# Shifting the up projections' split weights inside their buffers, by 16 bytes a tile in block 1 and 4 bytes a tile in block 2

## The chip, the cores and the metric

The kernel runs on one core of a Trainium2 chip. The metric is the device time of one execution in microseconds (us), the median of the timed runs. Engines are named as the profile names them: PE is TensorE (PEld its weight loads), DVE is VectorE, ACT is ScalarE, POOL is GpSimd, SP is SyncE, which here issues the weights' DMAs.

## What is computed

Two transformer blocks stand one behind the other, with 512 tokens, a width of 1024 and all data in float32. The first mixes forgetting attention with chunked gating, the second mixes latent attention with chunked attention under a modulated norm. Both end in the same kind of feed-forward part, and that is what the change touches:

```python
def conv_ffn(x, w_up, conv_w, conv_b, w_down):       # block 1; block 2 is alike
    h = x @ w_up                                     # 512 x 1024 @ 1024 x 5632
    h = lax.conv_general_dilated(h, ...) + conv_b    # causal, 3 taps, by channel
    a, g = jnp.split(h, 2, axis=-1)
    return (jax.nn.silu(g) * a) @ w_down             # 512 x 2816 @ 2816 x 1024
```

## The kernel before

Activations lie transposed, features on the 128 partitions and the 512 tokens along the free axis. Every large product is made of three matmuls in fp32r: an operand is split into a rounded part and a rest (`hi`, `lo`), and hi*hi, hi*lo and lo*hi are added up in one bank of PSUM.

**Weights.** `make_plan` writes down every piece of weights in the order of its use: what is loaded, whether POOL or DVE makes the rest, where the split goes, and a number called `skew`. `load_split` handles one piece: SP's DMA brings 128 x 1024 floats into `wraw`, ACT copies them into `whi` (line 345), DVE or POOL writes the rest into `wlo` (line 346). `whi` and `wlo` have four buffers each, 128 x 1088 floats, and the split starts `skew` floats into the buffer. A buffer is 4352 bytes long on each partition, 17 times 256, so the four buffers of each pool start at the same place modulo 256 bytes. The built program puts them and the activations `xnh`, `xnl` (tiles of 4096 bytes) at 128 modulo 256. `weights` takes pieces in the plan's order and keeps two more than the matmuls need loaded (`LOOK` = 2).

**Products by features** (`gemm_fm`: up, down, w_qk, w_lat). The weights are the stationary operand, 128 x 128 a matmul, and the activations the moving one, 512 columns wide. One output tile of the up projection is one piece of weights: 8 steps along k, 3 matmuls each. `ffn_up` goes over the tiles in pairs, j and j + 22. Its first two pairs are made in two halves of 256 columns, the other 40 tiles in full width. All of `gemm_fm`'s pieces have skew 0.

**Products by tokens** (`gemm_tm`). Here the activations are stationary and the weights move. Where a piece is under 384 columns wide, its skew is 48 floats, 192 bytes; otherwise it is 0.

PE's order is the order of the code; each matmul loads its own stationary operand, also where it is the same as the one before.

Of the kernel before, what the change touches and what calls it, by code (L numbers as in the profile page):

```python
# [231 lines left out]
class Kernel:  # L232
# [41 lines left out]
    def make_plan(self):  # L274
        i, plan = self.i, []

        def fm(name, tiles, kt0=0, nk=KT, pool=False, last=None):
            for n in tiles:
                for p in self.fm_pieces(i[name], n, kt0, nk):
                    plan.append((p, pool, None, 0))  # L280
            if last:
                plan[-1] = plan[-1][:2] + (last, 0)

        def tm(name, n, nk=KT, pool=True, last=None, per=None):
            skew = SKEW // 4 if n < 384 else 0
            for p in self.tm_pieces(i[name], n, nk, per):
                plan.append((p, pool, None, skew))
            if last:
                plan[-1] = plan[-1][:2] + (last, 0)

        def parts(name, dest):
            for p in range(4):
                for g in range(2):
                    plan.append((i[name][p, g], False, dest.get((p, g)), 0))

        def ffn(up, down, last=None):
            for j in range(NF):
                fm(up, [j, j + NF])
            fm(down, range(KT), 0, NF, last=last)

        tm("w_v", 512, pool=False, per=1)
        tm("w_g1", 264, pool=False)
        fm("w_qk", [0, 4])
        fm("w_qk", [1, 5])
        tm("w_g0", 256, pool=False)
        tm("w_u", 512)
        fm("w_qk", [2, 6], pool=True)
        fm("w_qk", [3, 7], pool=True)

        parts("w_out", {(3, 1): ("mx", "mix", "mix")})  # L310
        ffn("w_up", "w_down", ("cv", "cv", "cv"))
        fm("w_lat", range(3))
        tm("w_ck0", 256, pool=False, last=("one", "m0", "m1"))
        tm("w_cq0", 288)
        tm("w_cv0", 256)

        def mla(c):
            tm(f"w_q{c}", 384, 2, False)
            tm(f"w_kn{c}", 256, 1, False)
            tm(f"w_kv{c}", 256, 1, False)  # L320

        for j, w in enumerate(("w_cq1", "w_ck1", "w_cv1")):
            if j == 2:
                mla(0)
            tm(w, 256)
        mla(1)
        parts("w_out_2", {(3, 0): ("one", "m3", "m4"), (3, 1): ("one", "m0", "m1")})
        ffn("w_up_2", "w_down_2")
        self.plan, self.loaded, self.taken = plan, [], 0
        self.ada_left, self.pools, self.before = [], {}, []  # L330

# [1367 lines left out]
```

## Time and profile before

| what | value |
|---|---|
| timed runs | 1245.37, 1245.84, 1248.73 us; median 1245.84 |
| the profiled execution | 1248.05 us, of them 1245.1 us from the first to the last instruction |
| PE busy | 1206.6 us, 97% of the span, 6730 matmuls |
| DVE, ACT, POOL busy | 803.4, 536.7, 173.0 us |
| mean granted clock of PE | 0.989 |
| up projection in full width, block 1 and 2 | about 261 to 478 us and 903 to 1120 us |
| down projections in full width | about 478 to 583 us and 1120 to 1225 us |

A matmul's row in the timeline gives when it began and how long it took to the modelled end. Matmuls overlap, so the time that one costs is the distance between two starts, called the pitch below, and not the duration in the row. Over a stretch, the pitch is the length of the stretch by the count of matmuls in it.

### The profile page before, as it was taken

To read this page: it belongs to the slowest core of one execution; us is meant where nothing else is said; L and a number is where in the kernel's file an instruction comes from. 1 tells how busy PE (TensorE), PEld (TensorE's weight loads), DVE (VectorE), ACT (ScalarE), POOL (GpSimd) and SP (SyncE) were. 2 spreads that over 40 slices of the span, in tenths; PEclk is the share of its full clock that TensorE was granted. 3 is DMA by queue.
4 is the path that set the end of the run, shared out by engine and by line. 5 is a ranking of instruction groups with operands and counts; after the bars stand their busy time and mean duration, and the time that the engine had idled before them with its cause. 6 is when DMAs were issued, how large, how long until landed. Compare 5 with 4: busy or idle time off the path is not lost.

```text
span 1245.1 us, 17452 instructions
## 1 busy us (share of the span) xinstructions
PE 1206.6 (97%) x6730; PEld 1048.7 (84%) x6730; DVE 803.4 (65%) x1538; ACT 536.7 (43%) x963; POOL 173.0 (14%) x202
## 2 busy tenths in 40 slices
PE   9989999899999999999998998999999999999998
PEld 6878878888888888888998997889988888888887
DVE  6656887587877777533656889766676566563221
ACT  5534554354344343322534556564554444442110
POOL 1255401210000000000264332301200000000000
PEclk9989999999999999999998999999999999999999
DMA  7311222146555566533121222110132222233330
GB/s 239 105 65 52 85 68 68 52 144 206 179 184 189 196 199 191 181 93 114 56 94 42 73 83 76 35 35 18 59 119 93 102 102 86 101 93 102 118 110 17
DMA packets 40034, 131.58 MB, mean 106 GB/s; under 512 B 4608, under 2 KB 5504, under 8 KB 39952
## 3 DMA queue, kind: packets, MB, share of 16 engines
q1 hardware_dynamic: 31536, 102.64, 25.7%
q10 hardware_dynamic: 8208, 27.27, 6.7%
q8 instruction: 52, 0.85, 0.3%
q0 software_dynamic: 208, 0.57, 0.2%
q14 instruction: 30, 0.25, 0.1%
HBM read 128.37 MB, written 2.10 MB: 105 GB/s over the span
## 4 chain that ended last, share of the span: by engine, by line
PE 83%; DVE 8%; POOL 4%; ACT 3%; issue 2%; DMA 1%; SPq 0%; POOLq 0%; ACTq 0%; DVEq 0%
PE mm L367 73%; PE s L367 4%; PE o L367 3%; PE s L603 2%; POOL wlo L346 1%; DVE wlo L346 1%; DMA x<-in_xT_dram 1%; ACT p L594 1%; ACT whi L345 0%; PE s L694 0%; DVE s L590 0%; DVE kl L668 0%; DVE nw L522 0%; PE mm L1639 0%; POOL gelu L1081 0%
## 5 line engine op out<-in xcount | busy, mean ns | idle before, releaser
L367 PE MATMUL mm<-xnh,whi 128*128 128x512 f32 (+1 forms) x832 | 313.4, 377 | 3.2 <-DVE nt L550 3.2
L367 PE MATMUL mm<-xnl,whi 128*128 128x512 f32 (+1 forms) x832 | 312.5, 376 | 1.9 <-DVE xnl L562 1.3
L367 PE MATMUL mm<-xnh,wlo 128*128 128x512 f32 (+1 forms) x832 | 311.9, 375 | 0.0
L346 DVE TENSOR_TENSOR wlo<-wraw,whi 128x1024 fp32r<-128x1024 f32 (+4 forms) x175 | 200.6, 1155 | 167.1 <-ACT whi L345 166.2
L345 ACT CAST whi<-wraw 128x1024 fp32r<-128x1024 f32 (+4 forms) x194 | 191.5, 991 | 259.2 <-PE mm L367 214.3
L367 PEld LDWEIGHTS mm<-xnh,whi 128*128 128x128 f32 x832 | 157.9, 190 | 30.8 <-issue 3.8
L367 PEld LDWEIGHTS mm<-xnl,whi 128*128 128x128 f32 x832 | 158.0, 190 | 29.8 <-DVE xnl L562 1.5
L367 PEld LDWEIGHTS mm<-xnh,wlo 128*128 128x128 f32 x832 | 157.8, 190 | 27.6
L367 PE MATMUL mm<-gh,whi 128*128 128x512 f32 (+1 forms) x384 | 141.7, 369 | 1.1 <-DVE x L936 0.6
L367 PE MATMUL mm<-gh,wlo 128*128 128x512 f32 (+1 forms) x384 | 141.4, 368 | 0.0
L367 PE MATMUL mm<-gl,whi 128*128 128x512 f32 (+1 forms) x384 | 141.4, 368 | 0.0
L728 DVE SCALAR_TENSOR_TENSOR cv<-mm,cols,cv 128x510 f32<-128x510 f32 (+1 forms) x176 | 130.5, 746 | 2.9 <-ACT cv L726 1.4
L367 PE MATMUL mm<-whi,xnh 128*128 128x256 f32 (+3 forms) x304 | 97.1, 319 | 0.7 <-ACT vv L1045 0.6
L367 PE MATMUL mm<-wlo,xnh 128*128 128x256 f32 (+3 forms) x304 | 94.1, 310 | 0.3 <-DVE wlo L346 0.3
L367 PE MATMUL mm<-whi,xnl 128*128 128x256 f32 (+3 forms) x304 | 93.8, 309 | 0.1
L997 DVE CUSTOM_DVE_ANT_0 wada<-wada,cs,cols 128x1024 f32<-128x1024 f32 x48 | 61.5, 1281 | 38.8 <-DMA wada<-in_w_ada_dram 38.8
L367 PEld LDWEIGHTS mm<-gh,whi 128*128 128x128 f32 x384 | 72.4, 189 | 13.6 <-DVE x L936 0.8
L367 PEld LDWEIGHTS mm<-gl,whi 128*128 128x128 f32 x384 | 72.4, 189 | 12.0
L367 PEld LDWEIGHTS mm<-gh,wlo 128*128 128x128 f32 x384 | 72.4, 189 | 11.9
L594 ACT ACTIVATE p<-s,st 128x128 f32<-128x128 f32 (+1 forms) x96 | 50.6, 528 | 66.5 <-DVE st L590 50.8
L367 PE MATMUL mm<-mix,whi 128*128 128x256 f32 (+1 forms) x288 | 74.8, 348 | 3.8 <-ACT vm L1567 2.6
L743 ACT ACTIVATE cv<-cv 128x512 f32<-128x512 f32 x44 | 27.8, 632 | 114.8 <-DVE cv L728 114.8
(311 smaller groups left out, 1877.7 us busy)
## 6 DMA issues: line engine op xcount, KB each, us to landing
wraw<-in_w_up_dram SPq DMA_DIRECT2D x88, 512.0 KB, 3.4
wada<-in_w_ada_dram ACTq DMA_DIRECT2D x48, 512.0 KB, 3.6
wraw<-in_w_down_dram SPq DMA_DIRECT2D x32, 512.0 KB, 3.5
wraw<-in_w_out_dram SPq DMA_DIRECT2D x16, 512.0 KB, 3.4
wraw<-in_w_down_dram SPq DMA_DIRECT2D x16, 384.0 KB, 3.2
wraw<-in_w_qk_dram SPq DMA_DIRECT2D x8, 512.0 KB, 3.5
wraw<-in_w_v_dram SPq DMA_DIRECT2D x8, 256.0 KB, 4.8
x<-in_xT_dram SPq DMA_DIRECT2D x8, 256.0 KB, 6.0
```

The costliest lines, as they stand in the source:

```text
L345: nc.scalar.copy(hi[:, :n], raw[:, :n])
L346: (nc.gpsimd if pool else nc.vector).tensor_tensor(out=lo[:, :n], in0=raw[:, :n], in1=hi[:, :n].bitcast(F32), op=ALU.subtract)
L367: self.nc.tensor.matmul(out, lhsT, rhs, start=start, stop=stop, **kw)
L594: nc.scalar.activation(out=p[:, :nk], in_=s[:, :nk], func=AF.Exp, bias=st[:, len(parts) - 1:len(parts)], scale=-1.0, accum_out=hd["sums"](qi))
L603: self.nc.tensor.transpose(s[:, c], p[:, c], self.ident)
L728: nc.vector.scalar_tensor_tensor(out=t[:, d:], in0=ps[:, :512 - d], scalar=w[2 - d], in1=t[:, d:], op0=ALU.mult, op1=ALU.add)
L743: nc.scalar.activation(out=gate, in_=gate, func=AF.Silu)
L997: nc.vector.tensor_tensor_reduce(out=w, in0=w, in1=self.cs, scale=1.0, scalar=self.col("b_ada_2", n), op0=ALU.mult, op1=ALU.add, accum_out ...
```

## The change

`ffn` gets a `step`, and after the two pieces of a pair have been put into the plan it gives each a skew of its own. With t the tile's place in the order of use, 0 to 43, the skew is `step * t` modulo `16 * step` floats. Block 1 has step 4, so the split weights start at 0, 16, 32 ... 240 bytes and then at 0 again; block 2 has step 1, so they start at 0, 4, 8 ... 60 bytes. `whi` and `wlo` of a piece share the offset. Tiles 0, 16 and 32 keep offset 0. In the built program every engine has the same instructions in the same order with the same waits; only the addresses in `whi` and `wlo` differ. The raw weights, the activations, the down projections and every other product stay where they were.

```diff
-        def ffn(up, down, last=None):
+        def ffn(up, down, step, last=None):
+
             for j in range(NF):
                 fm(up, [j, j + NF])
+                for n in (-2, -1):
+                    plan[n] = plan[n][:3] + (step * (2 * j + 2 + n) % (16 * step),)
             fm(down, range(KT), 0, NF, last=last)
...
-        ffn("w_up", "w_down", ("cv", "cv", "cv"))
+        ffn("w_up", "w_down", 4, ("cv", "cv", "cv"))
...
-        ffn("w_up_2", "w_down_2")
+        ffn("w_up_2", "w_down_2", 1)
```

## Rows read from the trace of the kernel before

**Rows 1.** The page: span, busy time by engine, chain that ended last.

```profile
span 1245.1 us, 17452 instructions
...
PE 1206.6 (97%) x6730; PEld 1048.7 (84%) x6730; DVE 803.4 (65%) x1538; ACT 536.7 (43%) x963; POOL 173.0 (14%) x202
...
PE 83%; DVE 8%; POOL 4%; ACT 3%; issue 2%; DMA 1%; SPq 0%; POOLq 0%; ACTq 0%; DVEq 0%
```

**Rows 2.** Stretches: length, busy time (instructions) of PE, PEld, DVE, ACT, POOL, clock, DMA.

```profile
266.00:470.00 204.00, 204.00 (x902) 169.01 (x901) 164.18 (x227) 85.27 (x114) 0.00 (x0) 1.00 0.58 188
906.00:1110.00 204.00, 204.00 (x902) 169.01 (x901) 127.59 (x155) 90.49 (x116) 0.00 (x0) 1.00 0.29 100
482.00:580.00 98.00, 98.00 (x434) 81.21 (x433) 46.39 (x67) 30.29 (x47) 0.00 (x0) 1.00 0.49 148
```

**Rows 3.** Timeline of PE, up projection of block 1: start, duration (us), instruction.

```profile
300.17 0.39 PE L367 MATMUL mm<-xnh,whi 128*128 128x512 f32 x1
300.40 0.39 PE L367 MATMUL mm<-xnl,whi 128*128 128x512 f32 x1
...
302.21 0.39 PE L367 MATMUL mm<-xnh,whi 128*128 128x512 f32 x1
```

**Rows 4.** Timeline of PE, w_v, full width, just after a wait.

```profile
18.84 0.50 PE L367 MATMUL mm<-wlo,xnh 128*128 128x512 f32 x1 [0.26 <-DVE wlo L346]
19.18 0.39 PE L367 MATMUL mm<-whi,xnl 128*128 128x512 f32 x1
19.41 0.40 PE L367 MATMUL mm<-whi,xnh 128*128 128x512 f32 x1
19.64 0.40 PE L367 MATMUL mm<-wlo,xnh 128*128 128x512 f32 x1
...
21.26 0.39 PE L367 MATMUL mm<-whi,xnl 128*128 128x512 f32 x1
21.49 0.39 PE L367 MATMUL mm<-whi,xnh 128*128 128x512 f32 x1
21.71 0.39 PE L367 MATMUL mm<-wlo,xnh 128*128 128x512 f32 x1
```

**Rows 5.** Timeline of PE, down projection of block 1, halves of 256 columns, all offsets 0.

```profile
595.63 0.28 PE L367 MATMUL mm<-gl,whi 128*128 128x256 f32 x1
...
597.07 0.28 PE L367 MATMUL mm<-gl,whi 128*128 128x256 f32 x1
```

**Rows 6.** Timeline of PE, w_ck0, 256 columns, moving weights at 192 bytes.

```profile
628.54 0.28 PE L367 MATMUL mm<-whi,xnh 128*128 128x256 f32 x1
...
630.81 0.28 PE L367 MATMUL mm<-whi,xnl 128*128 128x256 f32 x1
```

**Rows 7.** Timeline of PE, w_cv0, 256 columns, moving weights at 192 bytes.

```profile
650.51 0.28 PE L367 MATMUL mm<-wlo,xnh 128*128 128x256 f32 x1
...
652.39 0.28 PE L367 MATMUL mm<-whi,xnl 128*128 128x256 f32 x1
```

**Rows 8.** Timeline of PE, w_out_2, 512 columns, moving operand 64 bytes off the weights.

```profile
761.06 0.63 PE L367 MATMUL mm<-mix,whi 128*128 128x512 f32 x2
761.53 0.39 PE L367 MATMUL mm<-mix,wlo 128*128 128x512 f32 x1
761.76 0.62 PE L367 MATMUL mm<-mix,whi 128*128 128x512 f32 x2
762.22 0.40 PE L367 MATMUL mm<-mix,wlo 128*128 128x512 f32 x1
```

**Rows 9.** Groups in 266:470: count, busy us, mean ns, idle before (us) and its releasers.

```profile
L367 PE MATMUL mm<-xnh,whi 128*128 128x512 f32 x300 | 116.8, 389 | 0.0
L367 PEld LDWEIGHTS mm<-xnh,whi 128*128 128x128 f32 x301 | 56.5, 188 | 11.6
L346 DVE TENSOR_TENSOR wlo<-wraw,whi 128x1024 fp32r<-128x1024 f32 x38 | 45.1, 1219 | 1.5 <-ACT whi L345 1.4
L345 ACT CAST whi<-wraw 128x1024 fp32r<-128x1024 f32 x38 | 39.8, 1046 | 50.5 <-PE mm L367 32.6 <-DVE mod L997 18.0
...
L728 DVE SCALAR_TENSOR_TENSOR cv<-mm,cols,cv 128x510 f32<-128x510 f32 x39 | 29.0, 745 | 0.0
L728 DVE SCALAR_TENSOR_TENSOR cv<-mm,cols,cv 128x511 f32<-128x511 f32 x37 | 27.7, 748 | 0.9 <-ACT cv L726 0.8
```

**Rows 10.** The same columns, ACT in 628:665, splits written at an offset of 192 bytes.

```profile
L345 ACT CAST whi<-wraw 128x1024 fp32r<-128x1024 f32 x6 | 6.2, 1047 | 8.4 <-DMA wraw<-in_w_cv_dram 4.6 <-PE mm L367 3.9
```

## The prediction

> **What bounds the kernel now.** I read the page first, then stretches, then single rows of PE. The page says that PE is busy for 97% of the span and holds 83% of the chain that ended last [rows 1]. The second question is whether the touched stages are limited by PE alone. In both up projections PE is busy for all of a 204 us stretch, at clock 1.00 throughout (2.4 GHz, the upper of its two levels), and its group by form has no idle time before it [rows 2, 9]. DVE works 164.2 of the 204 us in block 1 and 127.6 in block 2, ACT 85 and 90 [rows 2]. So nothing but the pitch of the matmuls sets the end here, and the change can act by the pitch alone, unless it makes another engine late.
>
> The third question is what a matmul costs. From 300.17 to 302.21 there are nine pitches: 2.04 / 9 = 0.2267 us [rows 3]. The stretch agrees: 902 matmuls touch 204 us, and since each row is 389 ns long about 1.7 of these began before it, so 204 / 900.3 = 226.6 ns, in both blocks and, by 98 us and 434, in the down projection [rows 2, 9]. At 2.4 GHz, 512 columns are 213.3 ns, so 13.3 ns more are paid a matmul.
>
> This pitch is a rhythm that PE falls into, not a fixed price. After a wait the starts in w_v go 19.18, 19.41, 19.64 ... 21.26: nine pitches of (21.26 - 19.18) / 9 = 231.1 ns; from 21.49 on the pitch is 0.22 to 0.23 us again and stays so [rows 4]. The bout costs 9 x (231.1 - 226.7) = 40 ns. Once found, the rhythm holds through both up projections, over all four weight buffers.
>
> And the rhythm depends on where the two operands lie. At 256 columns with all operands at the same place modulo 256 bytes, 12 pitches take 1.44 us, 120.0 ns [rows 5]. Where the weights are skewed by 192 bytes I find 20 pitches in 2.27 us, 113.5 ns, in one product [rows 6], and 16 in 1.88 us, 117.5 ns, in another with the same addresses modulo 256 [rows 7]. So an offset between the two reads can change a matmul by up to 6.5 ns, and the same offset can give two rhythms.
>
> **The change, part by part.** No instruction is added, removed or moved.
>
> The matmuls concerned: a block's up projection has 40 tiles in full width, 24 matmuls each, 960, and 4 tiles in halves, 4 x 24 x 2 = 192. Tiles 0, 16 and 32 keep offset 0, so 38 x 24 = 912 and 3 x 48 = 144 a block are shifted, 1824 and 288 in all. One ns of pitch on the full ones is 1.8 us of time, 0.15%.
>
> *Full width, in rhythm.* The moving operand, and with it its place in memory, is what it was; the stationary one is read within the 226.7 ns beside it, 188 ns a load, with idle time before it [rows 9]. At 512 columns I have no row with an offset and a long run. The nearest with equal operands is 226.7 [rows 3]. The only rows with an offset are in block 2's output projection, where the moving operand lies 64 bytes off the weights: 1.16 us from 761.06 to 762.22 for five pitches, 232 ns, but in a run broken by attention, in which equal operands show 231 too [rows 4, 8]. The floor is read from the slope: from 113.5 to 226.7 ns, 256 columns more cost 113.2 ns, so the best rhythm at 256 costs 0.443 ns a column and so does the one that the up projection has now. I read this as a price of streaming the moving operand with nothing on top; the 120.0 at 256 has 6.5 ns on top, the 231 to 232 some 4.4. An offset can take away only what is on top, and here there is nothing left. So the bounds are 0 and +4.4 ns a matmul, 0 to +8.0 us (1824 x 4.4), with a gain below 0 left to a rival. I take 0: the row with the same moving operand, the same width and an unbroken run is the 226.7 one.
>
> *Full width, at a change of tile.* Offsets differ between neighbouring tiles, so PE may have to find its rhythm anew 88 times. Bounds: nothing, as at every change of buffer now, or a bout of 40 ns each, 88 x 0.040 = 3.5 us [rows 4]. I take 1 us, nearer to nothing, since each step is 4 or 16 bytes, against the wait of [rows 4] that starts a bout.
>
> *Halves.* 288 matmuls at 120.0 ns may become 117.5 or 113.5, -0.7 or -1.9 us [rows 5 to 7]; or stay. I take -0.7.
>
> *ACT and DVE.* They write the splits at offsets that are no longer multiples of 64 bytes. ACT's copy takes 1047 ns at an offset of 192 bytes and 1046 at 0 [rows 9, 10]. DVE already writes at 4 and at 8 bytes past a tile's start in the convolution, 511 and 510 columns, in 748 and 745 ns [rows 9]. So 0. Cover, if that fails: DVE has 204 - 164.2 = 39.8 us idle in block 1's stretch, 1.05 us for each of its 38 splits of 1219 ns; they would have to become almost twice as long before PE waits [rows 2, 9].
>
> The sum: 0 + 1.0 - 0.7 + 0 = +0.3 us. The profiled execution took 1248.05 us, span 1245.1, and would take 1248.3; it stands 2.2 us above the median of the runs, 1245.84. Against that median I predict 1246.1 us.
>
> The skill has a rule on this. Under "Who interferes with whom", the Trainium skill's page "SBUF — State Buffer" gives TensorE two independent read ports, one for the moving operand and one for weight loads, and says that PE waits on nobody; by it an offset does nothing anywhere, and the sum would be 0. The trace does not bear out its general form, since 120.0 and 113.5 ns stand side by side for the same work at different offsets [rows 5, 6], but those are matmuls with hardly any time beside the load.
>
> **Rivals.**
>
> *The rhythm breaks (slower).* The 226.7 may need both operands at the same place modulo 256 bytes. At other offsets PE would stay in what [rows 4] show only in passing, 231.1 ns. For: the same offset of 192 bytes has two rhythms at 256 columns, the slower one 4 ns above the other over a run of 16 pitches [rows 6, 7]; the rows with an offset at 512 columns show 232 [rows 8]. Against: those come after interruptions, and at 512 columns the load has slack. Price 4.4 x 1824 = +8.0 us, less 0.7: 1253.1 us. It decides from the point at which more than half the offsets lose the rhythm: +4 us, 1249.8.
>
> *The offset takes something off (faster).* What helped the 256-column products by 2.5 to 6.5 ns [rows 5 to 7] may be an event a matmul, whatever its width. The pitch would fall to 224.2 or 220.2: 1824 x 2.5 = 4.6 us or 1824 x 6.5 = 11.9 us, and 0.7 to 1.9 in the halves; 1240.6 or 1232.1 us. Against it stands the slope above. For it: full columns at 2.4 GHz are 213.3 ns, so 13.3 remain to be explained, and I only inferred that they belong to the stream. It may hold for some offsets and not for others. The Trainium skill's page "TensorE: Matmul & The Clock Gate", under "Back-to-back issue gap", gives N / 2.4 + 2.5 ns, 215.8 at 512 columns; by it, as an estimate, 10.9 ns a matmul are there to be had, 19.9 us. No run of fp32r here comes near it.
>
> *The change is inert.* Hi and lo share their offset and the moving operand is fixed, so if only the moving stream sets the pitch nothing changes, in the halves either: 1245.8. This is in the forecast's band.
>
> **How the numbers follow.** The forecast with the inert case gets 0.50, the broken rhythm 0.32, the gain 0.18. The forecast's own band is 1245.8 - 1.9 = 1243.9 up to 1245.8 + 3.5 = 1249.3. About 0.3%, 3.7 us, is what a measurement of this kernel can tell from no change: below 1242.1 is faster, above 1249.5 slower. So same 0.50, slower 0.32, faster 0.18. The range for 8 in 10 is 1241 to 1254: it takes in the forecast, the whole price of the broken rhythm with room for the spread of runs, and of the gain only its weak edge; some 0.15 is left out below and 0.03 above.
>
> **What would show it.** Right: in both up projections some 902 matmuls touch a stretch of 204 us, and starts are 226 or 227 ns apart at every offset, with at most a few longer ones at a tile's start. Broken rhythm: about 885 in the stretch (204 / 231.1 + 1.7), and pitches between 224 and 236 within a tile, perhaps only at some offsets; block 1 and block 2 need not agree. A gain: 912 to 928 matmuls. ACT's row at 1046 ns and DVE's at 1219 would show the writes untouched. The forecast is wrong if PE shows idle time before whi or wlo, or if tiles with one offset have a pitch of their own.

## The result and the profile after

The changed kernel takes 1261.22 us (median of 1256.49, 1261.08, 1261.37 and 1261.82), the kernel before in the same comparison 1246.72: a ratio of 1.0099, 95% interval 1.0085 to 1.0113, or 12.3 us (10.6 to 14.1). It is slower by 1%, outside the range that I gave. The profiled execution took 1261.82 us, its span is 1260.1 us; 1245.1 before [rows 1].

The page of the changed kernel: span, busy time, and the chain that ended last.

```profile
span 1260.1 us, 17452 instructions
...
PE 1219.2 (97%) x6730; PEld 1051.4 (83%) x6730; DVE 804.8 (64%) x1538; ACT 538.3 (43%) x963; POOL 173.1 (14%) x202
...
PE 82%; DVE 8%; POOL 4%; ACT 3%; issue 2%; DMA 1%; SPq 0%; POOLq 0%; ACTq 0%; DVEq 0%
```

The same instructions, the same bound; PE is busy for 12.6 us longer. The stretches of [rows 2], the second one moved to where block 2's up projection now runs:

```profile
266.00:470.00 204.00, 204.00 (x882) 165.37 (x882) 163.10 (x223) 85.21 (x112) 0.00 (x0) 1.00 0.57 189
920.00:1124.00 204.00, 204.00 (x880) 164.92 (x879) 123.31 (x149) 85.69 (x111) 0.00 (x0) 1.00 0.29 100
482.00:580.00 98.00, 98.00 (x434) 81.14 (x433) 49.17 (x72) 30.45 (x48) 0.00 (x0) 1.00 0.46 142
```

Where 902 matmuls touched 204 us, 882 and 880 do, at the same granted clock of 1.00 and with no gap in PE's work. The down projection, whose weights did not move, keeps its 434 in 98 us. So the pitch has grown in the two up projections and nowhere else.

How much that costs in all is read from the chain that ended last. Its two longest pieces are unbroken work of PE: from block 1's up projection through the down projection, and the same in block 2. Columns: start (us), length (us), what, count. The third row shown is the piece just ahead of block 2's, 39 matmuls in halves. Before:

```profile
247.42 343.72 PE mm L367 x1599
...
883.35 4.78 PE mm L367 x39
...
891.78 341.21 PE mm L367 x1577
```

and after:

```profile
248.67 348.52 PE mm L370 x1599
...
891.63 6.23 PE mm L370 x39
...
901.51 346.42 PE mm L370 x1577
```

The same 1599 matmuls take 4.80 us more, the same 1577 take 5.21 us more: 10.0 us of the span's 15.0. The other 5.0 us lie outside these pieces, and 1.45 of them are in sight: the 39 matmuls in halves take 6.23 us instead of 4.78. The experiments come back to that.

The groups of 266 to 470 us, as [rows 9]:

```profile
L370 PE MATMUL mm<-xnh,whi 128*128 128x512 f32 x294 | 115.9, 394 | 0.0
L370 PEld LDWEIGHTS mm<-xnh,whi 128*128 128x128 f32 x294 | 55.2, 188 | 12.8
...
L349 DVE TENSOR_TENSOR wlo<-wraw,whi 128x1024 fp32r<-128x1024 f32 x37 | 44.2, 1218 | 2.8 <-ACT whi L348 2.6
L348 ACT CAST whi<-wraw 128x1024 fp32r<-128x1024 f32 x37 | 38.6, 1044 | 53.2 <-PE mm L370 53.2
```

A matmul's row is 394 ns long instead of 389, but a weight load is still 188 ns, and the splits are written in 1218 and 1044 ns (1219 and 1046 before). Writing at these offsets costs DVE and ACT nothing, and PE still has no idle time.

Last, the starts of neighbouring tiles in block 1, the first matmul of each. A tile is 24 matmuls, so the distance between two rows by 24 is the tile's mean pitch:

```profile
284.25 0.40 PE L370 MATMUL mm<-xnh,whi 128*128 128x512 f32 x1
...
289.85 0.39 PE L370 MATMUL mm<-xnh,whi 128*128 128x512 f32 x1
...
323.25 0.40 PE L370 MATMUL mm<-xnh,whi 128*128 128x512 f32 x1
...
328.71 0.39 PE L370 MATMUL mm<-xnh,whi 128*128 128x512 f32 x1
...
334.15 0.39 PE L370 MATMUL mm<-xnh,whi 128*128 128x512 f32 x1
...
339.60 0.39 PE L370 MATMUL mm<-xnh,whi 128*128 128x512 f32 x1
...
345.19 0.40 PE L370 MATMUL mm<-xnh,whi 128*128 128x512 f32 x1
```

The tile at 128 bytes: 289.85 - 284.25 = 5.60 us, 233.3 ns a matmul. The one at 240 bytes: 5.46, 227.5. At 0: 5.44, 226.7. At 16: 5.45, 227.1. At 32: 5.59, 232.9. Read in this way, every offset has a pitch that comes back each time it is used (mean ns in full width; the sequence of single pitches inside a tile repeats too):

| block 1, bytes | 16 | 32 | 48 | 64 | 80 | 96 | 112 | 128 | 144 | 160 | 176 | 192 | 208 | 224 | 240 | 0 |
|---|---|---|---|---|---|---|---|---|---|---|---|---|---|---|---|---|
| pitch | 227.0 | 233.0 | 233.2 | 233.1 | 231.8 | 233.9 | 233.1 | 233.4 | 233.4 | 233.0 | 229.8 | 229.1 | 233.1 | 233.3 | 227.5 | 226.7 |

| block 2, bytes | 4 | 8 | 12 | 16 | 20 | 24 | 28 | 32 | 36 | 40 | 44 | 48 | 52 | 56 | 60 | 0 |
|---|---|---|---|---|---|---|---|---|---|---|---|---|---|---|---|---|
| pitch | 232.3 | 230.9 | 229.7 | 233.4 | 232.7 | 231.1 | 234.8 | 233.3 | 234.3 | 233.4 | 230.4 | 233.3 | 233.0 | 233.1 | 230.4 | 228.1 |

More than half stand near 233.3, which is 6.7 ns above 226.7. At 0 and 240 the first few pitches are long (238, 232, 230 at 240 bytes; 230, 236, 229, 232, 231 at 0 in block 2) and then the rhythm of 226.7 is found again.

One thing stands out: 16 bytes costs nothing in block 1, where the tile ahead is at 0, and 6.7 ns a matmul in block 2, where the tile ahead is at 12.

### The profile page after: what moved, and what is told of

Its sections match the earlier page's. It is cut to its first block, busy times and chain, and to the rows that moved or that the text cites. A ratio compares the mean times of both kernels' runs of the same rounds, so it can differ in the third digit from the quotient of the medians.

```text
span 1260.1 us, 17452 instructions
## 1 busy us (share of the span) xinstructions
PE 1219.2 (97%) x6730; PEld 1051.4 (83%) x6730; DVE 804.8 (64%) x1538; ACT 538.3 (43%) x963; POOL 173.1 (14%) x202
## 4 chain that ended last, share of the span: by engine, by line
PE 82%; DVE 8%; POOL 4%; ACT 3%; issue 2%; DMA 1%; SPq 0%; POOLq 0%; ACTq 0%; DVEq 0%
PE mm L370 72%; PE s L370 4%; PE o L370 3%; PE s L606 2%; DVE wlo L349 1%; POOL wlo L349 1%; ACT whi L348 1%; ACT p L597 1%; DMA x<-in_xT_dram 0%; DVE nw L523 0%; DVE s L593 0%; DMA wraw<-in_w_g_dram 0%; DVE kl L671 0%; PE s L697 0%; PE mm L1642 0%
## 5 line engine op out<-in xcount | busy, mean ns | idle before, releaser
L370 PE MATMUL mm<-xnh,whi 128*128 128x512 f32 (+1 forms) x832 | 316.7, 381 | 3.2 <-DVE nt L553 3.2
L370 PE MATMUL mm<-xnl,whi 128*128 128x512 f32 (+1 forms) x832 | 316.0, 380 | 1.9 <-DVE xnl L565 1.3
L370 PE MATMUL mm<-xnh,wlo 128*128 128x512 f32 (+1 forms) x832 | 315.3, 379 | 0.0
```

What stands on the lines that cost most here:

```text
L370: self.nc.tensor.matmul(out, lhsT, rhs, start=start, stop=stop, **kw)
```

## The experiments

Three theories were set against each other. **A**: the pitch depends on the distance between the moving and the stationary operand, modulo 256 bytes, and on nothing else of the address. **B**: the change disturbs the clock, and that is part of the loss. **C**: it is the change of offset from tile to tile that costs, each tile having to find its rhythm anew. Spans are compared with the 1245.1 us of before; the pieces of the chain with 343.72 (1599 matmuls) and 341.21 (1577). In the first two kernels below, the block that is left alone has its piece back to 0.01 us; so one execution is enough to read a piece from, though not to compare totals.

### One block at a time

In one kernel only block 1's tiles keep their steps of 16 bytes, in the other only block 2's their steps of 4.

```diff
-                    plan[n] = plan[n][:3] + (step * (2 * j + 2 + n) % (16 * step),)
+                    plan[n] = plan[n][:3] + (skew(2 * j + 2 + n),)
```

with, for block 1 and for block 2 alone (in floats, by the tile's place t; the kernels below differ in this line),

```diff
+            skew = {"w_up": lambda t: 4 * (t % 16), "w_up_2": lambda t: 0}[up]
...
+            skew = {"w_up": lambda t: 0, "w_up_2": lambda t: t % 16}[up]
```

> The stagger of 16 bytes in block 1 alone. The changed kernel's span was 15.0 us longer: 4.8 us of it in block 1's up projection, 5.4 in block 2's, 4.8 elsewhere (1.3 at the start, the rest where the granted clock fell to half at other places). Theory A, the pitch: only block 1's up projection is slower, by 4.8 us, so about 1251.5 us against 1246.7. Theory B, the rest belongs to the change too (a later block 2 meets the clock's falls in another way): 1251.5 plus up to 4.8, about 1254 to 1256.

> The stagger of 4 bytes in block 2 alone. Theory A, the pitch: slower by 5.4 us, about 1252.1 us, with block 1's up projection back at 226.7 ns a matmul. Theory B, as in the run of block 1 alone: nothing ahead of block 2 is changed, so the clock's falls ahead of it stand where they stood and the time is 1252 as well; the two theories differ by the other run.

Block 1 alone: 1255.14 us, ratio 1.0068 (1.0045 to 1.0092). Block 2 alone: 1254.7 us, ratio 1.006 (1.0036 to 1.0084). The two long pieces of the chain, block 1 alone:

```profile
251.10 348.52 PE mm L370 x1599
...
899.31 341.21 PE mm L370 x1577
```

and block 2 alone:

```profile
249.34 343.71 PE mm L370 x1599
...
892.29 346.43 PE mm L370 x1577
```

Each block loses its own 4.80 or 5.22 us and the other block nothing. The two effects are independent and add up, to within 0.02 us of what the whole change costs in these pieces. A and C both want that. The timed differences, 8.5 and 7.5 us, lie above 4.8 and 5.2, though only block 1's interval (5.6 to 11.5 us) leaves its own piece out. Block 1's 1255.14 us falls where B had put it; block 2's 1254.7 is above the 1252 that both theories gave.

### Offsets that differ by 256 bytes

Every second tile of block 1 stands at 256 bytes, every second one of block 2 at 128.

```diff
+            skew = {"w_up": lambda t: 64 * (t % 2), "w_up_2": lambda t: 32 * (t % 2)}[up]
```

> Odd tiles of the up projections lie 256 bytes further in block 1, 128 bytes further in block 2. Theory A, the distance between the operands modulo 256 bytes sets the pitch: block 1 stays at 226.7 ns in every tile (902 matmuls in a stretch of 204 us) although each tile has another offset than the one before; block 2 has 233.4 ns in its odd tiles and, after some matmuls of 224 to 236, 226.7 in its even ones, together some 230.5. Theory C, it is the change of offset from tile to tile that costs: both blocks lose some 5 us alike.

```profile
249.13 343.72 PE mm L370 x1599
...
892.03 344.43 PE mm L370 x1577
```

One execution: 1250.51 us. Block 1's piece is 343.72 us, to the hundredth what it was: an offset that changes with every tile costs nothing, if it changes by 256 bytes. C falls for such changes; the next kernel, in which no offset changes, tests it for the others. Block 2 loses 3.22 us: its tiles at 128 bytes have 232.9 ns, those at 0 in between 227.4, with three long pitches each before the rhythm is found.

### One constant offset in all tiles

Block 1's 44 tiles all start at 128 bytes, block 2's all at 16.

```diff
+            skew = {"w_up": lambda t: 32, "w_up_2": lambda t: 4}[up]
```

> All 44 tiles of block 1's up projection start at one offset, 128 bytes, all of block 2's at one offset, 16 bytes. Distance theory: 128 bytes loses the rhythm in every tile, also with no change of offset between tiles: mean pitch 233 to 233.4 ns over block 1's full width, 960 x 6.5 = +6.3 us, some 877 matmuls touching 204 us. Block 2 settles what 16 bytes does: with the changed kernel it cost 0.3 ns in block 1, entered from offset 0, and 6.7 ns in block 2, entered from 12. If small distances are harmless in themselves, 226.7 and 0 us; if the rhythm at 16 bytes is only one that survives when it is carried over, 231 to 233.4 ns and +4 to +6.4 us. Rival (the cost is that of drifting offsets): 226.7 in both blocks, +0.

```profile
246.51 349.11 PE mm L370 x1599
...
898.95 347.46 PE mm L370 x1577
```

One execution: 1260.31 us. A constant 128 bytes costs 5.39 us (232.4 ns a matmul), a constant 16 bytes 6.25 us: 233.3 ns through all 40 tiles, although the changed kernel ran at 227.0 with the same 16 bytes in block 1. Offsets that never change from tile to tile cost as much as changing ones, so it is not the change that costs: C falls. And A needs an addition: the distance alone does not fix the pitch; what the pitch was before counts as well. The run entered from zero, below, tests that.

### Moving the other operand

Two small pads ahead of and behind the pool of activations move `xnh` and `xnl` by 64 bytes. In the first kernel the weights stay at 0, so the operands are 192 bytes apart; in the second all up tiles are put at 64 bytes too (the last line below, which is 0 in the first), and the distance is 0 again.

```diff
+        self.pool("pad_a").tile([P, 16], F32, name="pad_a")
         self.act = self.pool("act", 8)
+        self.pool("pad_b").tile([P, 48], F32, name="pad_b")
...
+            skew = {"w_up": lambda t: 16, "w_up_2": lambda t: 16}[up]
```

> Weights at offset 0 as in the kernel before; the activations' pool xnh, xnl and all that lies behind it is moved by 64 bytes, so the two operands are 192 bytes apart modulo 256. Distance theory: the up projections lose the rhythm although the weights stand where they were; 229 to 233.4 ns, +2.3 to +6.4 us a block, 875 to 892 matmuls in 204 us. Rival (only the place of the weights, or of the written split, modulo 256 counts): 226.7 ns, 902 matmuls, +0.

> The same move of the activations by 64 bytes, and the weights of all up tiles at offset 64 too, so the distance is 0 again. Distance theory: 226.7 ns, 902 matmuls in 204 us of both up projections, +0 there (other products, whose weights stay at 0, may lose). Rival (only the place of the weights counts): 231 to 233.4 ns as tiles at 64 bytes showed in the changed kernel, +4 to +6.4 us a block.

Activations alone moved, 1253.35 us in one execution:

```profile
247.29 345.72 PE mm L370 x1599
...
896.26 343.19 PE mm L370 x1577
```

Both moved, 1248.09 us:

```profile
249.41 343.71 PE mm L370 x1599
...
892.83 341.21 PE mm L370 x1577
```

With unmoved weights the up projections lose 2.00 and 1.98 us: 228.9 ns in full width, close to the 229.1 that the changed kernel showed at 192 bytes, the same distance. With both moved they lose nothing, with weights at 64 bytes, where the changed kernel had 233.1. At 64 bytes the place of the weights by itself is without effect; the distance between the two operands is what counts. The two kernels confirm this part of A, against the rival that only the place of the weights matters, in both directions.

### Only one part of the split

In block 1 `whi` is moved by 128 bytes and `wlo` stays at 0; in block 2 it is the other way round. Two of three matmuls load from `whi`.

```diff
-            hi = self.whi.tile([P, 1088], F32R, tag="whi", name="whi")[:, skew:]
-            lo = self.wlo.tile([P, 1088], F32R, tag="wlo", name="wlo")[:, skew:]
+            sh, sl = skew if isinstance(skew, tuple) else (skew, skew)
+            hi = self.whi.tile([P, 1088], F32R, tag="whi", name="whi")[:, sh:]
+            lo = self.wlo.tile([P, 1088], F32R, tag="wlo", name="wlo")[:, sl:]
...
+            skew = {"w_up": lambda t: (32, 0), "w_up_2": lambda t: (0, 32)}[up]
```

> Block 1: the rounded parts lie 128 bytes further, the rests at 0; block 2: the rests lie 128 bytes further, the rounded parts at 0. The order of matmuls is hi, hi, lo for each step along k. If each weight load disturbs the matmul that streams beside it by its own distance, two of three loads are off in block 1 and one of three in block 2, and the mean pitch is about 226.7 + 2/3 x 6.7 = 231.2 ns in block 1 and 228.9 in block 2. If the rhythm as a whole is lost or kept, both blocks are near 233.4 or both at 226.7.

```profile
250.02 349.98 PE mm L371 x1599
...
900.44 345.38 PE mm L371 x1577
```

One execution: 1259.72 us. With only `whi` off, block 1 loses 6.26 us, more than the 5.39 that it loses at a constant 128 bytes with both off. The pitches run 232, 233, 235 through every tile, as in this step of block 1:

```profile
276.50 0.39 PE L371 MATMUL mm<-xnh,whi 128*128 128x512 f32 x1
276.73 0.40 PE L371 MATMUL mm<-xnl,whi 128*128 128x512 f32 x1
276.97 0.40 PE L371 MATMUL mm<-xnh,wlo 128*128 128x512 f32 x1
277.20 0.39 PE L371 MATMUL mm<-xnh,whi 128*128 128x512 f32 x1
```

So the matmul with `wlo`, whose operands are at distance 0, is as late as the two others. Nor is it the load beside a matmul that counts alone: the next matmul's load begins within 0.01 us of each start, so `wlo`, at distance 0, is loaded beside the second matmul of a step, and that one takes 233 ns. With only `wlo` off, block 2 loses 4.17 us, in a sequence of 227, 232, 234. Neither "each load pays for itself" (231.2 and 228.9 ns) nor "one off, all at 233.4" holds in both blocks. The pitch belongs to the repeating sequence as a whole, not to the single matmul.

### Entered from the rhythm

In block 1 every second tile is at 0, so that each offset follows a tile at 226.7 ns. In block 2 the first five tiles, four in halves and one in full width, are at 0 and the other 39 at 16 bytes.

```diff
+            skew = {"w_up": lambda t: (t % 2) * (t // 2 if t < 34 else (32, 48, 56, 60, 62)[t // 2 - 17]),
+                    "w_up_2": lambda t: 0 if t < 5 else 4}[up]
```

> Block 1: every second tile at offset 0, the ones between at 8, 12, 16 ... 64, then 128, 192, 224, 240, 248 bytes, so that each offset is entered out of the 226.7 ns rhythm. Block 2: the four tiles in halves and the first in full width at 0, then all 39 others at 16 bytes. Theory (a rhythm that stands is kept at 16 bytes, and found anew only near 0): 16 bytes gives 226.7 to 227 ns in block 1 and in all of block 2, where the same constant 16 bytes without the first tile at 0 gave 233.3 (+0 us instead of +6.4); most other offsets 230 to 234 ns. Rival (block 1 and block 2 differ for another reason, and 16 bytes is lost in block 2 always): 233.3 there, +6.2 us.

```profile
248.06 345.75 PE mm L370 x1599
...
894.58 341.20 PE mm L370 x1577
```

One execution: 1249.68 us. Block 2's piece is 341.20 us: 39 tiles at 16 bytes cost nothing at all, all at 226.7 ns, where the same constant 16 bytes from the first tile on cost 6.25 us. In block 2 the only difference is the five tiles ahead. In block 1, tiles at 16, 0, 20 and then 0 again:

```profile
288.60 0.39 PE L370 MATMUL mm<-xnh,whi 128*128 128x512 f32 x1
...
294.04 0.39 PE L370 MATMUL mm<-xnh,whi 128*128 128x512 f32 x1
...
299.48 0.39 PE L370 MATMUL mm<-xnh,whi 128*128 128x512 f32 x1
...
305.08 0.39 PE L370 MATMUL mm<-xnh,whi 128*128 128x512 f32 x1
```

16 bytes: 5.44 us, 226.7 ns. 20 bytes: 5.60 us, 233.3 ns. The whole list, entered from 0:

| bytes | 8 | 12 | 16 | 20 | 24 | 28 | 32 | 36 | 40 | 44 | 48 | 52 | 56 | 60 | 64 | 128 | 192 | 224 | 240 | 248 |
|---|---|---|---|---|---|---|---|---|---|---|---|---|---|---|---|---|---|---|---|---|
| pitch | 230.8 | 226.7 | 226.7 | 233.1 | 231.0 | 226.7 | 233.1 | 226.7 | 226.7 | 230.7 | 233.1 | 233.2 | 233.6 | 233.0 | 233.3 | 232.9 | 228.9 | 233.0 | 226.7 | 233.3 |

At 12, 16, 28, 36, 40 and 240 bytes a standing rhythm is kept; in the changed kernel's block 2, where the tile ahead had already lost it, 12, 28, 36 and 40 had 229.7, 234.8, 234.3 and 233.4. At the other offsets it is lost wherever one comes from. I see no rule of the distance in the list of those that keep it.

### The rest: 10 us of work without any offset

All offsets are 0, and 44 matmuls that are overwritten by the next one are added, 23 in block 1's up projection and 21 in block 2's. So the two stages become as much longer as by the change, with the pitch unbroken.

```diff
+                        if k == 0 and n in extra:
+                            self.mm(o, wh, xh, True, True)
                         self.mm(o, wh, xh, k == 0, False)
```

> All offsets 0 as in the kernel before; 23 extra matmuls of 512 columns are put into block 1's up projection and 21 into block 2's, one ahead of a tile's first, which overwrites what they wrote. They cost 44 x 226.7 ns = +10.0 us in the same two stages in which the changed kernel loses its 4.84 + 5.35 = 10.2 us, with the pitch unbroken. The changed kernel's span is 15.0 us above before, and 4.8 of them lie outside the up projections, where the granted clock falls to half at other places. Theory (those 4.8 us are the ordinary spread of such falls, or follow from something else in the change): this kernel takes +10 us, 1257. Rival (they follow from the lengthening itself, since later stages come at another time): +13 to +15 us, 1260 to 1262.

1260.57 us, ratio 1.011 (1.0092 to 1.0128): 13.7 us, 11.5 to 16.0. Its chain, with the piece in halves ahead of block 2's:

```profile
246.89 348.93 PE mm L367 x1622
...
889.49 6.26 PE mm L367 x39
...
899.39 345.96 PE mm L367 x1598
```

The two pieces are 5.21 and 4.75 us longer, 10.0 us as worked out. The rest of the time is not in them, and no operand moved. So some 3.7 us (1.5 to 6.0) came on top when these two stages got 10 us longer without any offset, and the time lies in the range of the rival. The changed kernel's rest, 2.3 us by the timed runs (12.3 less 10.0) and 5.0 by the profiled one, need not come from the offsets either.

It can be seen in the clock. The 39 matmuls take 6.26 us here and 6.23 in the changed kernel, 4.78 before. Columns as in [rows 2], first the changed kernel's stretch, then this kernel's:

```profile
892.40:895.80 3.40, 3.40 (x19) 3.40 (x18) 0.00 (x0) 0.00 (x0) 0.21 (x1) 0.50 0.00 0
```

```profile
889.80:893.20 3.40, 3.40 (x19) 3.40 (x18) 0.00 (x0) 0.00 (x0) 0.66 (x1) 0.50 0.03 5
```

and the kernel before, from its last fall to the end:

```profile
792.30:1245.00 452.70, 445.54 (x2392) 384.53 (x2390) 241.91 (x378) 181.56 (x300) 16.70 (x22) 1.00 0.24 80
```

For 3.4 us at 892.4 and 889.8 the granted clock is 0.50, the lower of TensorE's two levels (1.2 GHz), and before it stays at 1.00 there. Ahead of it, PE does the same attention and the same halves with their waits in all three. Yet this is not a rule: a fall near 890 is also in the runs by 256 bytes, with constant offsets, with the activations moved and with only 64 bytes in the halves (below), and it is missing with block 1 alone, where the stage comes as late as here. Added up over all such stretches, the changed kernel's profiled run has 37.5 us at the lower level, the kernel before 27.3; half of the difference, 5.1 us, is, as an estimate, what work at full speed would have saved, near the 5.0 that were left.

The timed runs bear this out. Their spans (us), set side by side by the mean granted clock of the run:

| clock | before | changed | 10 us of work | 64 bytes in the halves (below) |
|---|---|---|---|---|
| 0.989 | 1245.1 to 1247.3, mean 1246.05 (12 runs) | 1254.7 | | 1243.0, 1243.1, 1243.1 |
| 0.988 | 1246.2, 1248.1 | | 1257.3, 1257.5, 1258.5 | 1246.0 |
| 0.985 | 1250.1, 1251.8 | 1259.3, 1259.4, 1260.1 | 1259.5 | 1247.0, 1249.2 |

At one clock the changed kernel is 8.7 us above before (means), and the kernel with 10 us of work 8.6 to 10.6: about what the pitch and the work cost, with nothing left over. So the rest comes and goes with the clock. Before stood at 0.989 or above in 24 of 28 runs, the changed kernel in one of four, the one with added work in none of five. Why stays open; longer stages alone do not explain it, since the kernel with 64 bytes in the halves, no stage of which is longer, stood there in only 5 of 12.

### Offsets only where they help

In halves of 256 columns an offset shortens the pitch. Two kernels give full width 0 and the pieces used in halves an offset: 64 bytes in block 1 and 192 in block 2 and in `w_lat`, as below, then 64 everywhere (16 floats in place of 48).

```diff
-                    plan[n] = plan[n][:3] + (step * (2 * j + 2 + n) % (16 * step),)
+            skew = {"w_up": 16, "w_up_2": 48}[up]
...
+                    plan[n] = plan[n][:3] + (skew if j < 2 else 0,)
             fm(down, range(KT), 0, NF, last=last)
+            for n in (-3, -2, -1):
+                plan[n] = plan[n][:3] + (skew,)
...
         fm("w_lat", range(3))
+        for n in (-3, -2, -1):
+            plan[n] = plan[n][:3] + (48,)
```

> Offsets where they may help instead: pieces used in full width at 0, pieces used in halves of 256 columns (the first 4 tiles of each up projection, the last of each down projection, w_lat) at 64 bytes in block 1 and 192 in block 2. Distance theory: full width keeps 226.7 ns (902 matmuls in 204 us); in the halves 120.0 ns falls to between 113.5 and 118: some 2 x (192 + 132) + 144 = 792 matmuls, -1.6 to -5 us, less what the change of tile costs. Rival (halves gain nothing that lasts): 0 us.

> Full width at offset 0; the pieces used in halves of 256 columns (first 4 tiles of each up projection, the last three pieces of each down projection, w_lat) at 64 bytes. In the run with 64 and 192 bytes, 64 gave the lower pitches: 115 to 117 ns where 0 gives 119.8. Some 800 matmuls x 3 to 4.8 ns = -2.4 to -3.8 us if they kept that everywhere; the halves of the earlier run together gained about 1.3 us only. Theory: -1 to -3 us, 0.1 to 0.2%, at the edge of what can be told. Rival (the gain is lost in waits and clock falls, as in the earlier run, whose one execution was 4.9 us above before): 0 or slower.

The first took 1250.02 us in its one execution, the second 1247.37 us, ratio 0.9996 (0.9979 to 1.0013). In the trace the halves do get shorter, from 120.0 ns to 117.8 at 192 bytes, and to 113.3 or 117.8 at 64; the long piece of block 2, which ends in such matmuls, is 340.50 us instead of 341.21:

```profile
894.77 340.50 PE mm L374 x1577
```

Summed over the halves that is some 3 us, an estimate. The timed totals show none of it (-2.6 to +1.6 us), but the table above does: at a clock of 0.989 and at 0.985 the second kernel's spans are some 3 us below those of before. A lower clock in most of its runs took this back, and in total no version beats the kernel before by more than can be told. The first kernel's one run had 0.985 and a span of 1248.3 us, below both spans of before at that clock, though its total is above.

## Why the prediction was wrong

**The bound: right.** PE's pitch sets the end in both up projections, DVE and ACT are as fast as before and PE never waits for them. All that the change did directly, it did through the pitch.

**"Full width, in rhythm. I take 0": this step failed.** Measured are 10.0 us in the two pieces on 1824 matmuls, 5.5 ns each. (The 40 tiles alone took 222.51 and 223.01 us instead of 217.63 in either block, 10.3 us or 5.6 ns each; the halves in the pieces became shorter.) The price lay beyond my upper bound too, 4.4 ns. Two arguments led there. The first was the floor: from 113.5 ns at 256 columns to 226.7 at 512 I read a slope without anything on top, and concluded that an offset has nothing to take away. That conclusion held, as no standing rhythm came below 226.7. But it speaks only against a gain, and I let it stand for "no change". The second was that at 512 columns the weight load has slack, 188 of 226.7 ns [rows 9]. It does, and its 188 ns did not change; yet with all this slack the distance between the two operands still set the pitch. With only `whi` off, even a matmul whose own operands are at distance 0 came late.

What I took as the nearest row was the unbroken run of [rows 3], because of the same width and moving operand. It differed in the one thing that the change touched. The only row with a distance between the operands at 512 columns was that of [rows 8], 232 ns, and I put it aside since it stood in a run broken by attention. It was within 1.3 ns of what most offsets then gave.

**The rival "the rhythm breaks": right in mechanism, too small in price.** It named the condition, both operands at the same place modulo 256 bytes; moving the activations, alone and with the weights, shows it. Its sign, some 885 matmuls in 204 us, came as 882 and 880. The condition is stricter than need be: at 12, 16, 28, 36, 40 and 240 bytes a rhythm that stands is kept. Its price of 4.4 ns came from a bout in which the rhythm is being found [rows 4]. A run that never finds it is slower: up to 234.8 ns, 233.3 at many offsets. With 5.5 ns instead of 4.4 it would have had 10.0 us instead of 8.0, with the rest on top.

**"At a change of tile", +1.0: within its bounds, but too large and of another kind.** A change of offset by 256 bytes costs nothing, so the change by itself is free. What there is at a tile's start is the return to 0 or 240 bytes: three to five long pitches, 20 to 26 ns a time, at 4 of 88 changes, 0.1 us in all. But at some offsets the tile ahead does decide the pitch, and with five tiles at 0 in front 16 bytes went from 6.25 us to nothing. I had not thought of a state that lasts for 40 tiles.

**Halves, -0.7: about right.** The last 48 matmuls in halves took 5.69 us in block 1 and 5.64 in block 2 instead of 5.76: 118.4 and 117.5 ns instead of some 120, by which 288 matmuls save 0.4 to 0.7 us, an estimate.

**What the sum did not have: the rest.** I carried the pitch's us to the total one to one. Between runs of the same granted clock that holds, but the clock was not the same: 10 us put into the same stages without any offset cost 13.7 (11.5 to 16.0), and the sum has no term for the clock. The chances that I gave went by 8 us for the broken rhythm, and my range ended at 1254; with the price of 10.0 and the rest of 3.7 the rival would have stood at 1259.5.

**The two rules named ahead.** The Trainium skill's page "SBUF — State Buffer", under "Who interferes with whom", says that PE waits on nobody and reads both operands through ports of their own. Measured at 512 columns is 226.7 ns at distance 0 and 233.3 at many others, with nothing changed but the distance between the two operands, so the rule does not hold in this form, and the measurement decides. The Trainium skill's page "TensorE: Matmul & The Clock Gate", under "Back-to-back issue gap", gives N / 2.4 + 2.5 ns for an isolated matmul, 215.8 at 512 columns as an estimate by it. In the unbroken runs of this case, with a weight load for each matmul, no distance had a standing pitch below 226.7.

## What to carry to other kernels

Where TensorE is the bound and fp32r matmuls of 512 columns with a load each run without a gap, put the moving operand and the stationary one at the same place modulo 256 bytes, or verify any other placing by the count of matmuls in a stretch: 882 instead of 902 in 204 us was the effect of the offsets. At 256 columns an offset of 64 or 192 bytes gave the shorter pitch. When an operation has a steady rhythm, bound a change of its inputs by the row that shares the changed property, even if that row is short and disturbed, and not by the undisturbed row that lacks it. And a stage that gets 10 us longer may move the total by more, since the granted clock moves too: spans of the kernel before go from 1243.2 us at 0.992 to 1251.8 at 0.985. So a forecast's range should not be cut to the sum of its terms, and effects of a few us are best compared between runs of one clock.

## What was not expected of the hardware

- At the same instructions and the same granted clock of 1.00, matmuls of 512 columns follow each other in 226.7 ns, in 233.3 at many distances of the two operands modulo 256 bytes, or in other patterns of up to 234.8. An offset of 256 bytes changes nothing.
- The rhythm has a memory. At 16 bytes both 226.7 and 233.3 ns lasted through some 40 tiles, whichever was there first. 12, 28, 36, 40 and 240 bytes keep a standing 226.7 as well; at 0 it was found anew within nine matmuls, mostly fewer, out of every pattern tried.
- A matmul with its operands at distance 0 is late too, if its neighbours' operands are not: 232, 233 and 235 ns in a step with only `whi` moved.
- At 256 columns the sign is the other way: 120.0 ns at distance 0, 113.3 or 117.8 at 64 bytes.
- At one mean granted clock the spans of the kernel before lie within some 2 us, and from clock to clock they move by several: 1245.1 to 1247.3 at 0.989, 1250.1 and 1251.8 at 0.985.
